# Later remainder splits, a merged frequency column, and attention's value product ahead of the output projection

## The chip, the cores and the metric

The kernel runs on one core of a Trainium2 chip. A core has a matrix engine (PE in the profile; its weight loads are listed apart as PEld), a vector engine (DVE), a scalar engine (ACT), a general engine (POOL), and SP, which here issues nearly all DMA transfers. The engines run side by side, each through its own instructions in order, and wait for one another on semaphores. Matmuls write to PSUM, from where DVE or ACT take the results away. The metric is the device time of one execution in microseconds; a time given for a kernel is the median of its runs.

## The reference

One encoder layer is applied to a prompt of 256 tokens and to a sample of 2048 tokens, both of width 1024, with the same weights. The inputs and outputs are float32:

```python
def encoder_layer(x, w_in, rpb, w_fourier, b_fourier, g_pre, g_na, g_f, w_out, g_post):
    h = rms_norm(x, g_pre)
    proj = h @ w_in                       # 1024 -> 6 * 512
    q, k, v, z_a, u_f, z_f = split(proj)
    y_a = neighbourhood_attention(q, k, v, rpb)
    y_f = fourier_mix(u_f, w_fourier, b_fourier)   # real part of a 2-D FFT, then 512 x 512
    mixed = concat([rms_norm(y_a, g_na) * silu(z_a), rms_norm(y_f, g_f) * silu(z_f)])
    out = mixed @ w_out                   # 1024 -> 1024
    return x + rms_norm(out, g_post)
```

Attention is local: tokens lie on a grid 64 wide, each query sees a window of 8 rows and 16 columns, with a bias from a table. There are 8 heads of 64.

## The kernel before, in words

**Arithmetic.** A float32 product is made of three faster passes. Each operand is split into a high part `h` (a rounded copy, made by ACT) and a remainder `l = x - h` (made by DVE); `mm3` (lines 171 to 173) then issues `h*h`, `h*l` and `l*h` into one PSUM accumulation.

**Stage 1, input projection.** First the value and Fourier columns of the first tokens, then a loop over 16 blocks `b` of 128 output columns for the prompt's 256 tokens (kinds z_f, z_a, k, q). In pass `b` of this loop, `b_raw(b + 2)` splits the weights of the block after next (ACT copy L577, DVE subtraction L578), `n_scale` and `n_sum` prepare operands of the sample, and `n_first(j)` splits operand `j` of the sample: one ACT copy (L444) and one DVE subtraction (L445) of 128 x 2048 elements. Then come 24 matmuls of 256 columns.

**The seven products.** The sample is projected by a scheme of seven products per 2 x 2 block in place of eight, so there are seven operands `j` = 0 to 6. `vu(0, ...)` runs it for the value and Fourier columns in 14 steps, in the order of `j` = 0, 0, 1, 1, 2, 2, 3, 3, 4, 4, 5, 5, 6, 6. Each step is 12 matmuls of 512 columns. `op_split(j)` (L493/L494) splits the weight side of operand `j`; `hooks` is a dictionary from step to further work of the other engines, put ahead of that step's matmuls: `n_first`, `rows_load`/`rows_square` (L305, squares of later token rows, on ACT, behind a DMA), `w_load`, `w_sums`, `a_split`. A step's results are added on DVE (L521). After `vu(0)` the rest of the sample's projection follows, then the second half of the sample.

**Stage 2, Fourier.** `stage2(gq, zg, c)` is called for `gq` 0 to 3 and `c` 0 to 4. It makes four small products of 64 columns each, one per `g`, into one PSUM tile `pab` of 256 columns (two PSUM buffers of tag `b` and one of tag `c` are used in turn). For `gq == 0` a further product with one column, the middle frequency, goes into its own tile `pny` of tag `a`; its weights are in the small constant `dnyq`. `split_ab` takes each tile away as high part and remainder (L997, L998, and L1012, L1014 for `c == 4`).

**Stage 3, attention with the Fourier half's output projection.** After the Fourier product `y` (L1258) there are 36 groups of queries, nine for each of four pairs of heads; group 0 of each nine is the prompt's. The loop runs over steps `k`. In step `k` the matrix engine issues, in this order: `transp` of group `k-2` (transposes the softmax weights into four PSUM tiles `ptb[0]` to `ptb[3]`, L1485, from where DVE and ACT copy them to SBUF, L1489), then `scores` of group `k` (L1179; one of its four tiles is `ptb[0]`). In even steps with a group `g`, the "long steps", two halves of an output projection tile follow: `f_mm(.., 0)` into `ptb[2]` and `f_mm(.., 1)` into `ptb[3]`, 12 matmuls of 512 columns each (L1425). `f_evac(.., 0)` takes `ptb[2]` away on DVE (L1459), `f_evac(.., 1)` takes `ptb[3]` away on ACT (L1456). Last comes `pv` of group `k-2`, the product of softmax weights and values (L1508), into a PSUM tile of tag `c` that has one buffer; DVE multiplies its result by the gate (L1528) and, in the next step after its transposes, ACT squares it (L1532, L1536). The softmax of a group runs on DVE (L1201, bias and maximum), ACT (L1206, exponentials) and POOL (L1213, normalisation) in the steps between.

The transposes fill `ptb[0]` and `ptb[1]` first and `ptb[2]` and `ptb[3]` after them:

```python
for b, ch in enumerate(g["ch"]):
    for j, c in enumerate(ch):
        for h in range(2):
            for y, (c0, nk) in enumerate(c):
                nc.tensor.transpose(ptb[2 * b + y][:nk, x:x + 64], ...)
```

**Stage 4** is the attention half's projection, the last norm and the residual.

**What sets the order.** On PE the order is that of the program throughout. On ACT, DVE, POOL and SP it is the program's order in stage 1 and from attention on (`manual_schedule(engines=MAN)`); in stage 2 and most of the Fourier product a planner orders these four.

Of the kernel before, what the change touches and what calls it, by code (L numbers as in the profile page):

```python
# [10 lines left out]
F32 = mybir.dt.float32  # L11
# [34 lines left out]
def constants():  # L46
    c = {}
    c["ident"] = np.eye(128, dtype=np.float32)
    n1 = np.arange(128)
    f1 = np.zeros((128, 128))  # L50
    for k1 in range(64):
        f1[:, 2 * k1] = np.cos(2 * np.pi * ((k1 * n1) % 128) / 128)
        f1[:, 2 * k1 + 1] = np.sin(2 * np.pi * ((k1 * n1) % 128) / 128) if k1 else (-1.0) ** n1
    c["f1"] = f1.reshape(32, 4, 128).transpose(1, 0, 2).reshape(128, 128)
    nrm = 1.0 / np.sqrt(2048 * 64)
    n2 = np.arange(16)
    d = np.zeros((128, 16, 128))
    for g in range(16):
        for kl in range(4):
            k1 = 4 * g + kl  # L60
            for k2 in range(16):
                if k1:
                    k = k1 + 128 * k2
                elif k2 < 8:
                    k = 128 * k2
                else:
                    k = 64 + 128 * (k2 - 8)
                co = np.cos(2 * np.pi * ((n2 * k) % 2048) / 2048) * nrm
                si = np.sin(2 * np.pi * ((n2 * k) % 2048) / 2048) * nrm
                ca = k2 * 4 + kl  # L70
                cb = 64 + ca
                r0 = (kl * 2) * 16 + n2
                r1 = (kl * 2 + 1) * 16 + n2
                if k1:
                    d[r0, g, ca] = co
                    d[r1, g, ca] = -si
                    d[r0, g, cb] = si
                    d[r1, g, cb] = co
                else:
                    r = r0 if k2 < 8 else r1  # L80
                    d[r, g, ca] = co
                    d[r, g, cb] = si
    c["d2"] = d
    dn = np.zeros((128, 4))
    dn[:16, 0] = ((-1.0) ** n2) * nrm
    dn[:, 2] = np.arange(128) % 32 != 0
    c["dnyq"] = dn
    n = np.arange(256)[:, None]
    k = np.arange(129)[None, :]
    ang = 2 * np.pi * ((n * k) % 256) / 256  # L90
    f256 = np.concatenate([np.cos(ang), np.sin(ang)], axis=1) / np.sqrt(256 * 64)
    c["f256"] = f256.reshape(4, 2, 32, 258).transpose(0, 2, 1, 3).reshape(128, 2, 258)
    f = np.arange(64)
    sl = np.arange(32)
    cs = np.zeros((128, 2, 64))
    for b in range(2):
        rows, cols = slice(64 * b, 64 * b + 64), slice(32 * b, 32 * b + 32)
        ang = 2 * np.pi * ((f[:, None] * sl[None, :]) % 64) / 64
        cs[rows, 0, cols] = np.cos(ang)
        cs[rows, 1, cols] = np.where(sl == 0, (-1.0) ** f[:, None], np.sin(ang))  # L100
    c["cs"] = cs
    cm = np.zeros((128, 2, 32))
    cs_ = np.zeros((128, 80))
    rm = np.zeros((128, 16))
    for p in range(128):
        half, i, qc = p // 64, p // 16 % 4, p % 16
        for b in range(2):
            cb = 2 * b + half
            ws = min(max(16 * cb + qc - 8, 0), 48)
            kc = KP0[cb] + np.arange(32)  # L110
            cm[p, b] = np.where((kc >= ws) & (kc < ws + 16), 0.0, BIG)
        for cb, j in ((0, slice(0, 24)), (1, slice(24, 56)), (3, slice(56, 80))):
            ws = min(max(16 * cb + qc - 8, 0), 48)
            kc = KC0[cb] + np.arange(KW[cb])
            cs_[p, j] = np.where((kc >= ws) & (kc < ws + 16), 0.0, BIG)
        j = np.array(ORD[half])
        rm[p, :11] = np.where((j >= i) & (j < i + 8), 0.0, BIG)
    c["cmask"] = cm.reshape(128, 64)
    c["csmask"] = cs_
    c["rmask"] = rm  # L120
    return {k: np.ascontiguousarray(v.astype(np.float32)) for k, v in c.items()}
# [54 lines left out]
def build(tc, A, O):  # L176
# [31 lines left out]
    invt = cst.tile([128, 18], F32, name="invt")  # L208
    invf = cst.tile([128, 18], F32, name="invf")
    inva = cst.tile([128, 18], F32, name="inva")  # L210
    dnyq = cst.tile([128, 4], F32, name="dnyq")
    cm = cst.tile([128, 80], F32, name="cm")[:, :64].rearrange("p (b x) -> p b x", b=2)


# [226 lines left out]
    def n_first(j):  # L441
        src = nq[((0, 0), (1, 0), (0, 0), (0, 1), "t3", (1, 0), (1, 1))[j]]
        h, l = bnew[0, j] = [k8(F32R, "x" + x) for x in "hl"]
        nc.scalar.copy(h, src)  # L444
        nc.vector.tensor_tensor(out=l, in0=src, in1=f_(h), op=ALU.subtract)  # L445
# [297 lines left out]
    for b in range(16):  # L743
        kind, blk = divmod(b, 4)
        if b < 10:
            wz_load(1)
        if b in (0, 2):
            n_load((b // 2, 1))
        if b == 10:
            op_load(0)  # L750
        if b == 12:
            op_load(1)
        if b < 14:
            b_raw(b + 2)
        if b < 8:
            x, y = divmod(b, 2)
            n_scale(None, *divmod(x, 2)[::-1], range(2 * y, 2 * y + 2))
        elif b < 12:
            n_sum(b - 8)
        if b in (3, 5, 12, 13):  # L760
            n_first((3, 5, 12, 13).index(b))
        if b > 13:
            op_split(b - 14)
        p = mmt(512)[:, :TP]
        wh, wl = wb.pop(b)
        for k in range(KC):
            mm3(nc, p, wh[:, k], wl[:, k], hp_[:, k], lp_[:, k], k == 0, k == KC - 1)
        o = st.tile([128, 256], F32, tag="f", name="f", bufs=3)
        if kind == 1:
            v = [(o, p)]  # L770
        elif kind == 3:
            v = [(o[:, 128 * x:128 * x + 128].rearrange("p (x r c) -> p r x c", x=2, c=16),
                  p[:, 128 * x:128 * x + 128].rearrange("p (r x c) -> p r x c", x=2, c=16)) for x in range(2)]
        else:
            v = [(o.rearrange("p (r b c) -> p b r c", b=2, c=32), p.rearrange("p (b r c) -> p b r c", b=2, c=32))]
        for d, i in v:
            nc.scalar.activation(d, i, AF.Silu if kind < 2 else AF.Copy, scale=-0.125 if kind == 3 else 1.0)
        if kind < 2:
            nc.sync.dma_start(zD[kind, blk * 128:blk * 128 + 128, :TP], o)
        else:  # L780
            nc.sync.dma_start((kD if kind == 2 else qD)[blk, :, :TP], o)
# [14 lines left out]
    def at(i, f, *a):  # L796
        hooks.setdefault(i, []).append(call(f, *a))

    for x in range(4, 7):
        at(3 * x - 12, n_first, x)  # L800
    for x in range(4):
        at(2 * x + 1, rows_load, x + 5)
        at(2 * x + 4, rows_square, x + 5)
# [19 lines left out]
    for i in range(16):  # L823
# [48 lines left out]
        for j in range(7):  # L872
# [28 lines left out]
            if sg == 0:  # L901
                x, y = divmod(7 * (pr - 1) + j, 14)
# [113 lines left out]
    def stage2(gq, zg, c):  # L1016
        m = int(c in (2, 3))
        np_ = 96 if c == 4 else 128
        x = (gq * 5 + c) % 3 == 2
        p = ps.tile([np_, 4, 64], F32, tag="c" if x else "b", name="pab", bufs=1 if x else 2)  # L1020
        for g in range(4):
            dft(p[:, g, :], c, [(zg[g], d2[gq // 2][:, (gq % 2) * 4 + g, m * 64:m * 64 + 64])])
        split_ab(gq, c, lambda a: a[:, :1024].rearrange("p (k q g l) -> p q g k l", k=16, q=4, g=4)[:, gq],
                 p.rearrange("p g (k l) -> p g k l", l=4))
        if gq == 0:
            p = ps.tile([np_, 1], F32, tag="a", name="pny")
            dft(p, c, [(zg[0], dnyq[:, m:m + 1])])
            split_ab(gq, c, lambda a: a[:, 1024:1025], p)
        if gq == 2:
            p = ps.tile([np_, 129], F32, tag="a", name="pup")  # L1030
            dft(p, c, [(up[:, t], f256[:, t, 129 * m:129 * m + 129]) for t in range(2)])
            split_ab(gq, c, lambda a: a[:, 1025:1154], p)
# [6 lines left out]
    def pq(m):  # L1039
# [7 lines left out]
        for b, p in enumerate(pp):  # L1047
            h, l = PQ[m][0][:, b], PQ[m][1][:, b]
            if m == 0:
                split_ps(h, l, p)  # L1050
                continue
            t = sm.tile([128, 512], F32, name="wt%d" % b)
            nc.scalar.copy(t, p)
            nc.scalar.dma_start(wr32[16 * b:16 * b + 16:4], t[::32])
            keep = dnyq[:, 2:3]
            nc.scalar.activation(h, p, AF.Copy, scale=keep)
            nc.vector.scalar_tensor_tensor(out=l, in0=p, scalar=keep, in1=h.bitcast(F32), op0=ALU.mult,
                                           op1=ALU.subtract)
# [514 lines left out]
    for k in range(2, len(G) + 2):  # L1573
# [32 lines left out]
        else:  # L1606
# [4 lines left out]
            if g:  # L1611
# [10 lines left out]
                    ys_mul(ftiles[x + 1])  # L1622
                if x < 16:
                    ys_load(ftiles[x + 2])
                f_mm(ftiles[x], 0)
            else:
                soft(p, 1)
# [20 lines left out]
                f_evac(ftiles[x], 1)  # L1648
        if pr < 3 and i == 7:
            mask_p(pr + 1)  # L1650
        pv(f)
        if k == 12:
            pq_.close()
        if k + 1 < len(G):
# [133 lines left out]
```

## Time and profile before

| what | value |
|---|---|
| median of 3 runs | 938.73 us (937.64 to 939.05) |
| the profiled execution's own time | 937.48 us |
| its span from first to last instruction | 935.7 us |
| PE / PEld / DVE / ACT / POOL busy | 925.3 / 774.5 / 669.9 / 469.8 / 332.0 us |
| granted TensorE clock | 0.999 |
| 16-block prompt loop ends, `vu(0)` begins | 121.5 us into the span |
| stage 2 begins | 553.2 us |
| the 17 long steps with their followers | 612.3 to 819.5 us |

A row of the timeline gives the start in the span, the duration (both us), engine, line, operation, `out<-in`, tile shape and count; in brackets the idle time of that engine before it and what ended it. Matmuls are pipelined: a 512-column matmul shows a duration of 389 ns, while the next one starts some 227 ns after it, so that distances between starts tell more than durations.

### The profile page before, as it was taken

The numbers are of one execution on the slowest core, as the hardware profiler recorded it, in microseconds if no ns is written. First come the engines' busy times: TensorE is split into PE (matmuls) and PEld (weight loads), VectorE is DVE, ScalarE is ACT, GpSimd is POOL, SyncE is SP. The second block draws the span as 40 slices with busy tenths as digits, with TensorE's granted clock in tenths as the row PEclk, the third lists the DMA queues.
The fourth block names the chain that finished last, engine by engine and source line by source line (L and its number), as shares of the span: only waits on it lengthen the run. The fifth ranks groups of instructions, "written<-read, shape, count | busy, mean of one in ns | idle before, by whom it ended". The sixth has DMA issues, their size and how long they took to land.

```text
span 935.7 us, 18895 instructions
## 1 busy us (share of the span) xinstructions
PE 925.3 (99%) x6790; PEld 774.5 (83%) x6790; DVE 669.9 (72%) x1308; ACT 469.8 (50%) x1038; POOL 332.0 (35%) x337
## 2 busy tenths in 40 slices
PE   9999999999999999999999999999999999999997
PEld 7889988888888888888888888978788887888886
DVE  6487997688864967597666645677665666659997
ACT  5856577623332743233334425667655666654443
POOL 3200002436650300363333200445456565525444
PEclk9999999999999999999999999999999999999999
DMA  9899777468573999758888789888779899879993
GB/s 323 329 360 400 217 253 281 158 246 314 201 288 151 352 400 359 265 209 316 294 310 286 273 287 309 295 262 257 245 248 274 264 300 283 255 237 377 341 340 128
DMA packets 144829, 264.04 MB, mean 282 GB/s; under 512 B 21784, under 2 KB 84632, under 8 KB 141984
## 3 DMA queue, kind: packets, MB, share of 16 engines
q1 hardware_dynamic: 144576, 262.81, 80.9%
q8 instruction: 54, 0.88, 0.4%
q14 instruction: 39, 0.32, 0.1%
q10 hardware_dynamic: 160, 0.02, 0.0%
HBM read 174.75 MB, written 95.35 MB: 289 GB/s over the span
## 4 chain that ended last, share of the span: by engine, by line
PE 94%; DMA 3%; DVE 2%; issue 1%; ACT 0%; DVEq 0%; SPq 0%
PE mm L172 18%; PE mm L173 18%; PE mm L171 17%; PE ptb L1425 10%; PE po L1425 10%; PE pv L1508 5%; PE ptb L1485 3%; PE s L1179 3%; PE pab L1005 2%; PE ptb L1179 2%; DMA woD<-wo 1%; PE py L171 1%; PE py L173 1%; PE py L172 1%; PE pf L1425 1%
## 5 line engine op out<-in xcount | busy, mean ns | idle before, releaser
L171 PE MATMUL mm<-xh,wa 128*128 128x512 f32 x448 | 174.4, 389 | 0.0
L173 PE MATMUL mm<-xh,wa 128*128 128x512 f32 x448 | 174.3, 389 | 0.0
L172 PE MATMUL mm<-xl,wa 128*128 128x512 f32 x448 | 174.3, 389 | 0.0
L548 POOL TENSOR_TENSOR ws<-wr 128x512 f32<-128x512 f32 x16 | 22.2, 1386 | 259.3 <-DMA wr<-wz 246.2
L171 PEld LDWEIGHTS mm<-xh,wa 128*128 128x128 f32 x448 | 84.1, 188 | 17.5
L173 PEld LDWEIGHTS mm<-xh,wa 128*128 128x128 f32 x448 | 84.1, 188 | 17.4
L172 PEld LDWEIGHTS mm<-xl,wa 128*128 128x128 f32 x448 | 84.1, 188 | 17.4
L1425 PE MATMUL po<-w,yh 128*128 128x512 f32 x280 | 86.8, 391 | 0.0
L1425 PE MATMUL ptb<-wo,yh 128*128 128x512 f32 x272 | 86.7, 400 | 0.0
L1213 POOL TENSOR_SCALAR w<-w,m 128x352 f32<-128x352 f32 (+4 forms) x136 | 75.4, 572 | 30.4 <-PE s L1179 14.0
L563 DVE TENSOR_TENSOR wa<-wr,wa 128x512 fp32r<-128x512 f32 x60 | 57.7, 969 | 30.6 <-ACT wa L562 30.3
L1206 ACT ACTIVATE w<-w,m 128x352 f32<-128x352 f32 (+4 forms) x136 | 69.9, 521 | 12.5 <-DVE m L1201 12.1
L861 DVE TENSOR_TENSOR f<-u,mm 128x512 f32<-128x512 f32 x64 | 43.6, 681 | 34.1 <-PE mm L173 29.5
L172 PE MATMUL mm<-vl,xh 128*128 128x512 f32 x168 | 65.6, 390 | 0.4 <-DVE vl L494 0.4
L171 PE MATMUL mm<-vh,xh 128*128 128x512 f32 x168 | 65.4, 389 | 0.0
L173 PE MATMUL mm<-vh,xl 128*128 128x512 f32 x168 | 65.4, 389 | 0.0
L1425 PEld LDWEIGHTS ptb<-wo,yh 128*128 128x128 f32 x272 | 49.3, 188 | 14.8 <-ACT sqa L1536 3.4
L1425 PEld LDWEIGHTS po<-w,yh 128*128 128x128 f32 x280 | 52.3, 188 | 11.0
L562 ACT CAST wa<-wr 128x512 fp32r<-128x512 f32 x60 | 36.5, 617 | 42.7 <-PE mm L173 16.8
L1508 PEld LDWEIGHTS pv<-pt,v 96*64 96x64 f32 (+2 forms) x1280 | 45.2, 137 | 11.6 <-issue 6.6
L1425 PE MATMUL po<-w,yl 128*128 128x512 f32 x140 | 54.5, 389 | 0.0
L1425 PE MATMUL ptb<-wo,yl 128*128 128x512 f32 x136 | 53.1, 391 | 0.0
(249 smaller groups left out, 2192.3 us busy)
## 6 DMA issues: line engine op xcount, KB each, us to landing
wr<-wz SPq DMA_DIRECT2D x48, 512.0 KB
vl<-sD SPq DMA_DIRECT2D x20, 512.0 KB
xm<-xm SPq DMA_DIRECT2D x9, 1024.0 KB
oD<-ofs SPq DMA_DIRECT2D x18, 512.0 KB
of<-oD SPq DMA_DIRECT2D x18, 512.0 KB
yr<-yD SPq DMA_DIRECT2D x34, 256.0 KB
zD<-f SPq DMA_DIRECT2D x16, 512.0 KB
woD<-wo SPq DMA_DIRECT2D x16, 512.0 KB
```

The costliest lines, as they stand in the source:

```text
L171: nc.tensor.matmul(out, lh, rh, start=first, stop=False)
L172: nc.tensor.matmul(out, lh, rl, start=False, stop=False)
L173: nc.tensor.matmul(out, ll, rh, start=False, stop=last)
L562: nc.scalar.copy(o[:, 0], src)
L563: nc.vector.tensor_tensor(out=o[:, 1], in0=src, in1=o[:, 0].bitcast(F32), op=ALU.subtract)
L861: nc.vector.tensor_tensor(out=dst(f, b), in0=src(uu[u]), in1=src(p), op=op)
L1179: nc.tensor.matmul(sp[2 * b + h][64 * y:64 * y + 64, j * w:(j + n) * w], g["q"][hs, 128 * b + 64 * y:128 * b + 64 * y + 64], kk[hs, k:k + ...
L1206: nc.scalar.activation(w, w, AF.Exp, bias=m[:, h:h + 1], scale=-1.0, accum_out=m[:, 2 + h:3 + h])
L1213: nc.gpsimd.tensor_scalar(w, w, m[:, 4 + h:5 + h], 1.0, ALU.mult, ALU.mult)
L1425: nc.tensor.matmul(p, (d["l"] if x == 2 else d["h"])[:, c], w(n, int(x == 1), c), start=j == 0, stop=j == 11)
L1485: nc.tensor.transpose(ptb[2 * b + y][:nk, x:x + 64], g["w"][b][ys, h, c0:c0 + nk], ident[ys, ys])
L1508: nc.tensor.matmul(p[hs, b, o], v[:nk, b, x, hs], g["pt"][b][:nk, h, j * 128 + o.start:j * 128 + o.stop], start=first, stop=last)
```

## The change

Three edits that do not depend on one another.

1. **Remainder splits.** `n_first(2)` moves from pass 12 of the prompt loop to pass 13. `n_first(3)` moves from pass 13 to step 1 of `vu(0)`. `n_first(4)`, `(5)` and `(6)` move from steps 0, 3 and 6 of `vu(0)` to steps 4, 7 and 10.
2. **Middle frequency.** The constant `dnyq` grows from 128 x 4 to 128 x 2 x 66 and now holds the 64 columns of `d2` for `g == 0`, the middle frequency as 65th column, and the mask column. The order of `g` is reversed, so that `g == 0` comes last in the `pab` tile, and for `gq == 0` its product has 65 columns instead of 64. The tile `pny` and its matmuls are gone; `split_ab` takes column 256 of `pab` instead.
3. **Values ahead of the projection.** In long steps `pv(f)` stands between the scores and `f_mm(.., 0)`; in the others it stays at the end.

```diff
-        if b in (3, 5, 12, 13):
-            n_first((3, 5, 12, 13).index(b))
+        if b in (3, 5, 13):
+            n_first((3, 5, 13).index(b))
...
-    for x in range(4, 7):
-        at(3 * x - 12, n_first, x)
+    for x in range(3, 7):
+        at(3 * x - 8 if x > 3 else 1, n_first, x)
...
-        p = ps.tile([np_, 4, 64], F32, tag="c" if x else "b", name="pab", bufs=1 if x else 2)
-        for g in range(4):
-            dft(p[:, g, :], c, [(zg[g], d2[gq // 2][:, (gq % 2) * 4 + g, m * 64:m * 64 + 64])])
+        p = ps.tile([np_, 260], F32, tag="c" if x else "b", name="pab", bufs=1 if x else 2)
+        for g in range(3, -1, -1):
+            s = 64 * (3 - g)
+            if gq == 0 and g == 0:
+                dft(p[:, s:s + 65], c, [(zg[g], dnyq[:, m, :65])])
+            else:
+                dft(p[:, s:s + 64], c, [(zg[g], d2[gq // 2][:, (gq % 2) * 4 + g, m * 64:m * 64 + 64])])
...
         if gq == 0:
-            p = ps.tile([np_, 1], F32, tag="a", name="pny")
-            dft(p, c, [(zg[0], dnyq[:, m:m + 1])])
-            split_ab(gq, c, lambda a: a[:, 1024:1025], p)
+            split_ab(gq, c, lambda a: a[:, 1024:1025], p[:, 256:257])
...
                 if x < 16:
                     ys_load(ftiles[x + 2])
+                pv(f)
                 f_mm(ftiles[x], 0)
...
-        pv(f)
+        if k % 2 or not g:
+            pv(f)
```

## Prediction before the run

> **What bounds the kernel now.** I read the page's shares and its chain first, then the busy time by stretch, then the timeline around each edited place.
>
> ```profile
> PE 925.3 (99%) x6790; PEld 774.5 (83%) x6790; DVE 669.9 (72%) x1308; ACT 469.8 (50%) x1038; POOL 332.0 (35%) x337
> PE 94%; DMA 3%; DVE 2%; issue 1%; ACT 0%; DVEq 0%; SPq 0%
> ...
> 613.78:820.30 206.52, 206.07 (x3001) 167.09 (x2997) 134.69 (x499) 131.70 (x416) 114.94 (x179) 1.00 0.87 265
> ```
>
> The matrix engine sets the end: 94% of the chain runs through it, and in the stretch of the long steps (last row: window, its length, then the busy time of PE, PEld, DVE, ACT, POOL) it is busy for 206.07 of 206.52 us. So edit 3, which only reorders that work, can win at most 0.45 us there, and what it can lose is open. Work on other engines counts only where PE comes to wait for it. The three edits touch three separate stretches, so their effects add.
>
> **Edit 3, values ahead of the projection.** This is the largest term. In the old order, one long step and what follows it look like this (PE, then ACT, then the group of all such ACT instructions):
>
> ```profile
> 707.18 0.39 PE L1425 MATMUL ptb<-wo,yl 128*128 128x512 f32 x1
> 707.50 1.59 PE L1508 MATMUL pv<-pt,v 96*64 96x128 f32 x40
> 709.02 0.91 PE L1485 MATMUL ptb<-ident,w 64*128 64x64 f32 x24
> 709.86 0.51 PE L1179 MATMUL s<-kk,q 64*64 64x352 f32 x4
> ...
> 707.60 0.69 ACT L1456 ACTIVATE ofs<-ptb,invf 128x512 f32<-128x512 f32 x1 [1.37 <-PE ptb L1425]
> ...
> L1456 ACT ACTIVATE ofs<-ptb,invf x17: 687/687/687, 619.5 to 818.0; 128x512 f32<-128x512 f32 x17
> ```
>
> The last projection matmul starts at 707.18 and ends at 707.57. Its result is in `ptb[3]`. ACT starts to take it away at 707.60 and is done at 708.29, always 687 ns later, 17 times of 17; ACT sat idle before, so it cannot be earlier. That is 0.79 us after the first value product (707.50). The transposes of the next step write `ptb[3]` again, so they must wait for that evacuation; in the old order the value product of 1.52 us (707.50 to 709.02) lies between and hides it entirely.
>
> In the new order the value product stands ahead of the projection, and the transposes come right behind `f_mm(.., 1)`. That cover is gone. What is left as cover is the first half of the transposes, which go to `ptb[0]` and `ptb[1]`. The 24 transposes take 0.84 us (709.02 to 709.86), the first 12 some 0.42 us. So PE stops for 0.79 + 0.06 - 0.42 = 0.43 us, with 0.06 for the release (the lag is measured below). PE is the bound, and the engine is in order: scores, values and the next step stand behind the waiting transpose, so the stop is lost. Groups with fewer key rows have less cover:
>
> ```profile
> 732.26 0.69 PE L1485 MATMUL ptb<-ident,w 64*96 64x64 f32 x16
> 732.88 0.44 PE L1179 MATMUL s<-kk,q 64*64 64x264 f32 x4
> ...
> 611.05 1.31 PE L1425 MATMUL pf<-wo,y0h 128*128 128x512 f32 x5
> 612.29 0.46 PE L1485 MATMUL ptb<-ident,sc 64*128 64x64 f32 x8
> 612.68 0.66 PE L1179 MATMUL s<-kk,q 64*64 64x256 f32 x8
> ```
>
> With 16 transposes (0.62 us) half is 0.31, and the wait is 0.54; with 8 (0.39 us) half is 0.20, the wait 0.65. The long steps are k = 2, 4, ... 34, seventeen; the transposes behind them are of groups 1, 3, ... 33. Of these two are prompt groups (9, 27; 8 transposes), four lie at the upper edge (1, 11, 19, 29; 16), eleven are full. Sum: 11 x 0.43 + 4 x 0.54 + 2 x 0.65 = 8.2 us.
>
> For the lag between another engine's end and PE's next start there are two rows:
>
> ```profile
> 673.99 0.08 DVE L1201 DVE_READ_ACCUMULATOR2_ANT m<- 128x1 f32 x1
> 674.22 0.68 PE L1485 MATMUL ptb<-ident,w 64*96 64x64 f32 x16 [0.41 <-DVE m L1201]
> ...
> 117.47 1.24 DVE L578 TENSOR_TENSOR wl<-wr,wh 128x1024 fp32r<-128x1024 f32 x1
> 118.77 0.39 PE L173 MATMUL mm<-ph,wl 128*128 128x256 f32 x1 [0.20 <-DVE wl L578]
> ```
>
> DVE's accumulator ends at 674.07, and the transposes that waited start at 674.22: 0.15. A subtraction ends at 118.71 and the matmul starts at 118.77: 0.06. The first is the same instruction as here. With 0.15 in place of 0.06 the sum is 17 x 0.09 = 1.5 us larger, 9.7. I take 8.9, the middle.
>
> The switch from projection to transposes costs the same as that to values: 0.32 us from the last matmul's start, 707.18 to 707.50; the single place where transposes already follow a projection tile shows 0.33 (five matmuls from 611.05 at some 0.23 put the last start near 611.97, transposes at 612.29). So the reordering alone is neutral: up to the next transposes PE changes from one kind of work to another four times in either order.
>
> Does the value product start late in its new place? It needs the copied transposes and its single PSUM buffer, freed by ACT's squares of the previous group.
>
> ```profile
> 713.97 0.39 ACT L1536 ACTIVATE sqa<-pv 128x256 f32<-128x256 f32 x1
> 714.13 0.73 PE L1425 MATMUL ptb<-wo,yh 128*128 128x512 f32 x2
> ```
>
> In step 18 the squares end at 714.36, 0.23 us after PE is through with the scores (714.13, where the projection starts now); with the lag 0.28 us. Projection matmuls never needed that buffer. Step 18 has the shortest scores of the long steps, so this is the worst case; I take 0.3 us for all steps together. DVE's `f_evac(.., 0)` moves back by 1.5 us, and with it the reciprocals behind it and POOL's normalisation:
>
> ```profile
> 705.56 2.44 POOL L1213 TENSOR_SCALAR w<-w,m 128x264 f32<-128x264 f32 x4
> 712.59 0.26 PE L1485 MATMUL ptb<-ident,w 64*96 64x64 f32 x2
> ```
>
> POOL ended that at 708.0, and the transposes that need it came at 712.59: a slack of 4.6 us hides it. The store of the values goes out earlier on SP's queue, ahead of the projection's store, and delays nothing that is needed within the step. Edit 3: **+9.2 us** (8.2 to 10.0).
>
> The Trainium skill, "Perfetto Trace Analysis", section "Matmuls", speaks against this order: independent matmul groups should rotate through PSUM banks so that the evacuation of one overlaps the next group's matmuls. The new order goes back to the bank just filled. Taken alone, without the transposes into the other two tiles, the rule would expose the whole 0.84 us, 17 times, 14.3 us; by the rows half of that is covered.
>
> **Edit 1, remainder splits.** At the end of the prompt loop DVE is late, and PE stops at each pass:
>
> ```profile
> 118.29 0.28 PE L172 MATMUL mm<-pl,wh 128*128 128x256 f32 x1
> 121.50 0.39 PE L171 MATMUL mm<-vh,xh 128*128 128x512 f32 x1
> 122.11 0.50 PE L172 MATMUL mm<-vl,xh 128*128 128x512 f32 x1 [0.21 <-DVE vl L494]
> ...
> 118.61 2.31 DVE L445 TENSOR_TENSOR xl<-nx,xh 128x2048 fp32r<-128x2048 f32 x1
> 120.81 4.65 DVE L494 TENSOR_TENSOR vl<-vr,vh 128x1024 fp32r<-128x1024 f32 x4
> ...
> 141.88 1.05 ACT L305 ACTIVATE xm<-xm 128x1024 f32<-128x1024 f32 x1
> 149.49 1.98 ACT L493 CAST vh<-vl 128x1024 fp32r<-128x1024 f32 x2
> 152.49 1.06 ACT L305 ACTIVATE xm<-xm 128x1024 f32<-128x1024 f32 x1 [1.01 <-DMA xm<-xm]
> ...
> 144.10 2.29 DVE L445 TENSOR_TENSOR xl<-nx,xh 128x2048 fp32r<-128x2048 f32 x1 [2.60 <-ACT xm L305]
> 152.16 2.36 DVE L494 TENSOR_TENSOR vl<-vl,vh 128x1024 fp32r<-128x1024 f32 x2
> ...
> 154.66 0.39 PE L171 MATMUL mm<-vh,xh 128*128 128x512 f32 x1
> ```
>
> Matmuls of 256 columns follow at 0.12 us, so 118.29 to 118.77 holds a stop of 0.36 us (remainder of weights, 117.47); 121.50 to 122.11 and the next start hold 0.38 + 0.11. Without the two `n_first` of 2.2 us, DVE has the weights of pass 15 at 116.5 and the first of `op_split(0)` near 119.8. These stops go: -0.9 us. The stop in pass 14 stays, since DVE still has `n_sum(3)` ahead of it.
>
> But the splits come back where DVE has no room. Operand 6 is needed in step 12. That step started at 154.66 and would now start at 153.8, its first matmul with the remainder 0.45 later, at 154.2. From 144.10 to 154.4 DVE had no idle time: remainder 6 (144.10), two additions, `op_split(5)`, four additions, `op_split(6)` (152.16, 2.36 us). In the new order remainder 5 takes the place of remainder 6, one addition of 0.6 us moves into the idle 2.60 us ahead of 144.10, and remainder 6 comes behind `op_split(6)`, which ends at 153.9. It takes 2.2 us, to 156.1, and PE gets it at 156.2: a wait of 2.0 us. Net **+1.1 us**.
>
> There is a worse form. The old remainder 6 did not start when its ACT copy ended (141.88) but at 144.10, when the squares queued behind the copy were done: its wait named those squares. In step 10 the new order again has squares behind the copy, and they wait for a transfer (152.49). ACT's copy would end at 153.3, the squares at 155.4, remainder 6 at 157.7: a wait of 3.5 us, net +2.6. Remainders 4 and 5 had no such wait; the nearest row, the same instruction, had it. I take +2.0 us, with -0.9 (no wait in step 12 at all) and +2.6 as the ends.
>
> **Edit 2, the merged column.**
>
> ```profile
> 553.99 0.34 PE L1005 MATMUL pny<-dnyq,zg 128*128 128x1 f32 x2
> 554.18 1.08 PE L1005 MATMUL pab<-d,zg 128*128 128x64 f32 x8
> 558.16 0.24 PE L1005 MATMUL pny<-dnyq,zg 128*32 128x1 f32 x6
> 558.33 0.43 PE L1005 MATMUL pab<-d,zg 128*128 128x64 f32 x2
> ...
> 555.08 0.41 DVE L997 CAST abh<-pab 128x256 fp32r<-128x256 f32 x1
> 555.52 0.42 DVE L998 TENSOR_TENSOR abl<-pab,abh 128x256 fp32r<-128x256 f32 x1
> 555.86 0.15 DVE L998 TENSOR_TENSOR abl<-pny,abh 128x1 fp32r<-128x1 f32 x1
> ```
>
> The removed products hold PE for 554.18 - 553.99 = 0.19 us each (0.26 for the fourth, with a short wait), the last, of six narrow ones, for 0.17: 1.0 us in all. A 65th column is nothing beside the weight load that sets the pace. But DVE starts late (555.08) and needs about 0.95 us for each tile's high part and remainder, and the three `pab` buffers now come free only when the extra column is out too (555.86, 0.15). The fourth tile needs the first one's buffer at 555.84 and gets it at 556.06, the fifth needs the second's: of 1.0 us I keep 0.5. Bounds: 0 and -1.0. **-0.5 us**. The larger constant, 67 KB instead of 2, goes out some 350 us earlier.
>
> The Trainium skill, "TensorEngine Tiling (Array Packing)", section "Instruction Overhead", gives a matmul a floor of about 60 cycles; by it the fourteen removed ones would be worth an estimated 0.35 us. The trace, with about 0.1 us for each, decides.
>
> **Sum.** 9.2 + 2.0 - 0.5 = +10.7 us. On the profiled execution, 937.48 us around a span of 935.7, that is 948.2. The median of the runs shown stands 1.25 us above that execution, which would make 949.4. I forecast **949 us**. The forecast's own range, from 8.2 - 0.9 - 1.0 on 937.5 to 10.0 + 2.6 on 938.7: 943.8 to 951.3.
>
> **Rivals.**
>
> *The evacuation stays hidden (other side).* If the transposes behind the projection did not have to wait for `ptb[3]`, edit 3 would cost only its 0.3 us or nothing. What decides is whether ACT ends within 0.42 us of the last projection matmul; for it speaks the place at 612.29, where transposes follow a projection tile without a stop (that tile lies in another PSUM buffer, though); against it the 0.79 us, seventeen times of seventeen. With edit 1 at -0.9, edit 2 at -1.0 and 0.3 left of edit 3, 937.5 - 1.6 = 935.9, 937 with the runs' offset: 8%. With edit 1 at +2.0 and edit 2 at -0.5, 938.7 + 1.8 = 940.5, or no change where edit 1 costs less: 5%.
>
> *The wait sits ahead of all transposes.* If the release is attached to the first transpose of a step and not to the first that writes `ptb[3]`, nothing covers the 0.84 to 0.94 us: 17 x 0.9 = 15.3 us, 955 in all. The first transposes need nothing of that evacuation, which speaks against it. 7%.
>
> *The softmax gets late instead.* Projection and softmax share DVE, so moving `f_mm` back might make the normalised weights late two steps on, and PE would stop there as well, by up to the 1.5 us of the shift where POOL is full (at the four ends of a pair of heads: +6 us). The slack of 4.6 us speaks against it; 4%, 955 or more.
>
> The forecast has 76%. Faster by over 0.2%, about what a measurement of this kernel can tell from no change: 8%; within 0.2%: 5%; slower: 87%. The range that leaves out no more than two in ten, and lets the first two rivals in part of the way, is 942.5 to 954.
>
> **What would show it.** In the changed profile, each long step should end with transposes right behind L1425, and in their middle a gap of 0.4 to 0.6 us on PE, released by ACT L1456, some 9 us in total. Around 154 there should be one wait of 2 us or more in the twelfth step of `vu(0)`, released by DVE L445, and no stop at 118.3 or 121.5. Stage 2 should start its second quarter about half a microsecond earlier after its own start. The prediction is wrong if the waits of PE on L1456 sum to less than 5 us, or if the transposes show no gap.

## The result and the profile after

The changed kernel takes **969.52 us** (965.49 to 973.8, four runs) against 938.45 us for the kernel before beside it: a ratio of 1.0329, 95% interval 1.0302 to 1.0356. It is slower, as forecast, but by 31 us where 10.7 had been summed. The profiled execution took 967.28 us around a span of 965.5. In the changed file the lines of the prompt loop and of `vu` stand one later, those of attention three later: L445 is L446, L1456 is L1459, L1485 is L1488, L1425 is L1428, L1508 is L1511.

First the page: engine totals, and the granted clock in 40 slices of 24 us.

```profile
PE 940.9 (97%) x6776; PEld 785.3 (81%) x6776; DVE 668.0 (69%) x1308; ACT 469.8 (49%) x1038; POOL 332.1 (34%) x337
...
PEclk9999999999999999999999978999999999999999
```

PE is less densely busy (97% for 99%), and there is something that no step of the prediction had: around the 24th slice the matrix engine's clock was not fully granted. The view by stretch says where (window, length, busy time and count of PE, PEld, DVE, ACT and POOL, then the granted clock, the DMA share and GB/s):

```profile
157.50:164.50 7.00, 3.89 (x11) 2.77 (x10) 7.00 (x6) 2.95 (x7) 6.30 (x3) 0.76 0.15 55
561.30:567.20 5.90, 4.87 (x61) 4.58 (x59) 4.97 (x17) 3.14 (x5) 0.52 (x1) 1.00 0.73 259
567.20:587.70 20.50, 20.50 (x143) 19.60 (x142) 6.13 (x18) 5.11 (x16) 1.26 (x1) 0.50 0.85 300
631.65:850.10 218.45, 210.84 (x3005) 169.33 (x2997) 132.77 (x499) 131.75 (x416) 113.63 (x179) 1.00 0.82 250
```

Three stretches carry the loss. In the twelfth step of `vu(0)` PE worked 3.89 of 7 us, half of that time at half clock. Stage 2 began at 561.3 us, PE stood still for a sixth of its first 5.9 us, and then the clock was at half for 20.5 us. The long steps take 218.45 us where the row of before had 206.52; there the clock is full. Compared start by start with the trace of before, PE is 8.1 us late at the start of stage 2, 17.9 at its end, 29.8 after the long steps, and it stays there. Of the 8.1 us, 2.2 had arisen by 102 us, ahead of every edited place; there the profiled executions of all kernels of this study lie between -0.7 and +2.2 us around that of before, whether or not they hold an edit ahead of stage 2, so that this part is not put down to the change.

The waits of PE (what waited, on what: us in total, times, the longest):

```profile
PE ptb L1488 <- ACT ofs L1459: 4.9, 17, 0.5
PE mm L174 <- DVE xl L446: 3.1, 1, 3.1
PE ptb L1428 <- issue: 2.2, 1, 2.2
...
PE mm L173 <- DVE vl L491: 1.3, 1, 1.3
```

The first row is the predicted one, seventeen times. Its 4.9 us is a lower figure than what was lost, since the modelled ends of the matmuls overlap the wait; the starts say more. In the third, PE stops for 2.4 us by starts at 825 us, between two projection matmuls. "Issue" names nothing that it waited for, but the trace has a load of instructions there (queue q8, 16 KB, 825.40 to 826.41), and PE goes on at 827.69, 1.28 us after its end. The timeline of one long step and its follower, PE and then ACT:

```profile
743.66 0.39 PE L1428 MATMUL ptb<-wo,yl 128*128 128x512 f32 x1
743.99 0.63 PE L1488 MATMUL ptb<-ident,w 64*128 64x64 f32 x13
744.83 0.53 PE L1488 MATMUL ptb<-ident,w 64*72 64x64 f32 x11 [0.22 <-ACT ofs L1459]
...
744.09 0.69 ACT L1459 ACTIVATE ofs<-ptb,invf 128x512 f32<-128x512 f32 x1 [2.62 <-PE ptb L1428]
```

ACT takes the bank away from 744.09 to 744.78; the transposes stop in their middle and go on at 744.83, 0.05 us later. The distances between starts at these seventeen places exceed the usual one by 0.40 to 0.64 us, 8.0 us in sum.

Two places of `vu(0)`, PE, DVE and POOL of the changed kernel:

```profile
150.48 0.39 PE L172 MATMUL mm<-vh,xh 128*128 128x512 f32 x1
152.17 0.50 PE L173 MATMUL mm<-vl,xh 128*128 128x512 f32 x1 [1.30 <-DVE vl L491]
157.75 0.39 PE L173 MATMUL mm<-vl,xh 128*128 128x512 f32 x1
161.25 0.80 PE L174 MATMUL mm<-vh,xl 128*128 128x512 f32 x1 [3.11 <-DVE xl L446]
161.84 0.63 PE L172 MATMUL mm<-vh,xh 128*128 128x512 f32 x1
162.27 0.63 PE L173 MATMUL mm<-vl,xh 128*128 128x512 f32 x1
...
148.09 2.29 DVE L446 TENSOR_TENSOR xl<-nx,xh 128x2048 fp32r<-128x2048 f32 x1 [3.63 <-ACT xh L445]
157.83 3.36 DVE L446 TENSOR_TENSOR xl<-nx,xh 128x2048 fp32r<-128x2048 f32 x1
...
159.12 3.21 POOL L549 TENSOR_TENSOR ws<-ws,wr 128x512 f32<-128x512 f32 x1
```

The tenth step waits 1.46 us for `op_split(5)`, which stood behind remainder 5 (148.09). The twelfth waits 3.27 us for remainder 6. Behind that wait matmuls of 512 columns follow at 0.43 us instead of 0.23: the clock is at half, for 3.4 us from 161.0. The stops at 118.3 and 121.5 are gone.

Stage 2's first tiles:

```profile
563.69 0.39 PE L1006 MATMUL pab<-dnyq,zg 128*128 128x65 f32 x2
564.69 0.85 PE L1006 MATMUL pab<-d,zg 128*128 128x64 f32 x6 [0.61 <-DVE abl L999]
565.38 0.39 PE L1006 MATMUL pab<-dnyq,zg 128*128 128x65 f32 x2
...
566.84 3.51 PE L1006 MATMUL pab<-d,zg 128*128 128x64 f32 x17 [0.42 <-PE pab L1006]
```

By starts the fourth column tile waits 0.77 us for its bank and the first tile of the second quarter 0.49. After that seventeen matmuls take 3.51 us, where the row of before at 558.33 had two in 0.43 and about 0.11 us from one to the next: half clock.

### The profile page after: what moved, and what is told of

It is laid out like the page before. It is cut to its first block, busy times and chain, and to the rows that moved or that the text cites. A ratio compares the mean times of both kernels' runs of the same rounds, so it can differ in the third digit from the quotient of the medians.

```text
span 965.5 us, 18877 instructions
## 1 busy us (share of the span) xinstructions
PE 940.9 (97%) x6776; PEld 785.3 (81%) x6776; DVE 668.0 (69%) x1308; ACT 469.8 (49%) x1038; POOL 332.1 (34%) x337
## 4 chain that ended last, share of the span: by engine, by line
PE 44%; DMA 6%; SPq 2%; DVE 2%; ACT 2%; issue 1%; POOL 1%; DVEq 0%; POOLq 0%; ACTq 0%
PE po L1428 10%; PE ptb L1428 8%; PE pv L1511 4%; PE mm L174 3%; PE mm L172 3%; PE mm L173 3%; PE pab L1006 2%; PE ptb L1488 2%; DMA wr<-wz 2%; PE s L1182 2%; DMA mt<-tr 2%; PE ptb L1182 1%; ACT ofs L1459 1%; PE py L172 1%; PE py L174 1%
## 5 line engine op out<-in xcount | busy, mean ns | idle before, releaser
L1428 PE MATMUL ptb<-wo,yh 128*128 128x512 f32 x272 | 87.0, 400 | 2.2 <-issue 2.2
L1428 PE MATMUL po<-w,yh 128*128 128x512 f32 x280 | 86.7, 391 | 0.0
L564 DVE TENSOR_TENSOR wa<-wr,wa 128x512 fp32r<-128x512 f32 x60 | 59.7, 1001 | 36.1 <-ACT wa L563 36.1
L1428 PEld LDWEIGHTS po<-w,yh 128*128 128x128 f32 x280 | 52.3, 188 | 11.0
L1428 PEld LDWEIGHTS ptb<-wo,yh 128*128 128x128 f32 x272 | 49.4, 188 | 12.9 <-issue 2.5
L1511 PEld LDWEIGHTS pv<-pt,v 96*64 96x64 f32 (+2 forms) x1280 | 45.2, 137 | 11.7 <-ACT sqa L1539 6.3
L1428 PE MATMUL po<-w,yl 128*128 128x512 f32 x140 | 54.5, 389 | 0.0
L1428 PE MATMUL ptb<-wo,yl 128*128 128x512 f32 x136 | 53.1, 390 | 0.0
```

The lines of the kernel that those rows point to most:

```text
L564: nc.vector.tensor_tensor(out=o[:, 1], in0=src, in1=o[:, 0].bitcast(F32), op=ALU.subtract)
L1428: nc.tensor.matmul(p, (d["l"] if x == 2 else d["h"])[:, c], w(n, int(x == 1), c), start=j == 0, stop=j == 11)
L1511: nc.tensor.matmul(p[hs, b, o], v[:nk, b, x, hs], g["pt"][b][:nk, h, j * 128 + o.start:j * 128 + o.stop], start=first, stop=last)
```

## The experiments

The theory after this profile: the three edits add; edits 1 and 2 each make PE stop, and the stops take the clock down; edit 3 loses what was predicted. Each run below was timed beside the kernel before (938.05 to 938.75 us in the four sets).

**One edit at a time.** Three kernels hold one edit each, as in the diff above.

> Edit 1 alone: the four norms one after the other at later steps of the remainder pass, the rest as before. Additive theory: the stops at 118 and 121 us are gone (-0.9), the tenth step waits about 1.5 us for its split, the twelfth about 3.3 us for the sixth remainder's low half, and the granted clock drops to half for one stretch of about 3.4 us behind that wait, which costs about 1.6 more: 4 to 6 us slower than before, 942.5 to 945. Prediction's theory: +2.0, 940.5, with no drop of the clock. Rival (the early slowdown is the rows' or the constants' changed layout, not this edit): within 1 us of before.

Measured: 945.14 us, 1.007 (1.0044 to 1.0097). Edit 1 alone, PE's timeline:

```profile
149.97 0.50 PE L172 MATMUL mm<-vl,xh 128*128 128x512 f32 x1 [1.65 <-DVE vl L490]
...
159.05 0.79 PE L173 MATMUL mm<-vh,xl 128*128 128x512 f32 x1 [3.10 <-DVE xl L445]
```

and the view by stretch behind the second wait:

```profile
157.90:164.70 6.80, 5.65 (x13) 4.46 (x14) 6.80 (x7) 2.28 (x4) 5.21 (x3) 0.50 0.21 80
```

Both waits are there (1.81 and 3.26 us by starts), and the clock is at half for 6.8 us from 157.9, of which 5.7 lie behind the second wait and cost half of that, 2.8 us. With the stops of 0.95 us gone: 1.81 + 3.26 + 2.8 - 0.95 = 6.9. The additive theory had the places right and the size 1 to 3 us too low.

> Edit 2 alone: the groups of a column tile in reverse order, the middle frequency's column as the 65th of the last group's matmuls, the constant grown from 4 to 132 columns. Additive theory: two waits of 0.6 to 0.8 us in the first two quarters of the second stage, and then the granted clock at half for about 20 us, which costs 9 to 10: about 948. Rival (the half clock needs the phase that edit 1's delay gives, since the window of the clock runs free): the waits of 1.4 us in sum alone, no half clock in the second stage, 939 to 940.5. Prediction's theory: -0.5, 938.2.

Measured: 951.71 us (947.79 to 955.41), 1.0139 (1.0092 to 1.0186). Edit 2 alone, PE's timeline and then the view by stretch:

```profile
556.81 0.85 PE L1006 MATMUL pab<-d,zg 128*128 128x64 f32 x6 [0.61 <-DVE abl L999]
...
558.97 8.48 PE L1006 MATMUL pab<-d,zg 128*128 128x64 f32 x57 [0.42 <-PE pab L1006]
```

```profile
553.00:595.40 42.40, 41.14 (x335) 37.31 (x333) 19.89 (x60) 16.65 (x38) 1.77 (x2) 0.76 0.71 236
```

The kernel before has full clock over the same stretch:

```profile
553.00:595.40 42.40, 42.40 (x406) 39.38 (x405) 24.70 (x83) 23.20 (x54) 6.35 (x9) 1.00 0.92 312
```

In edit 2 there are the same two stops, 0.78 and 0.49 us by starts, and half clock from 558.8 to 579.3 us (0.76 over this stretch). Edit 1 is not needed for it, so that rival falls. The four runs had mean granted clocks of 0.979 to 0.987, the slower ones the lower clocks: how long the clock stays down varies.

> Edit 3 alone: in long steps the value products go out ahead of the projection. Prediction's theory: the 17 waits of the transposes on ScalarE's evacuation, 8.0 us, and 0.3 to 1.4 us of value products that wait for their bank: 947 to 949, with a granted clock of 1.0 in the attention. Rival (with all edits together the attention slowed by 11.9 us because the stages before had left another phase of the queues): less than 6 us slower than before.

Measured: 948.71 us, 1.0112 (1.0082 to 1.0142), clock full in attention. The losses of the three, 7.1 + 13.7 + 10.7 = 31.4 us, agree with the 31.1 of the whole change: the edits add, as far as runs tell of which those with edit 2 spread over 8 us.

**Is it the bank?** Edit 3 with the projection's second half in another bank:

```diff
+        elif n:
+            p = ps.tile([128, 512], F32, tag="a", name="pf", bufs=3)
         else:
-            p = ptb[2 + n]
+            p = ptb[2]
```

> Edit 3 with one more change: the projection's second half is accumulated in a bank of the three that the scores use, not in the transposes' last bank. If the waits come from that bank being reused, as predicted, the 17 waits on ScalarE's evacuation are gone and the time is about 8 us under edit 3 alone: 939 to 941, less what the scores lose by having one bank fewer for a while (up to 3 us). Rival (the transposes wait since values ahead of the projection put the next softmax's products late, whatever bank): within 2 us of edit 3 alone.

Measured: 941.07 us, 1.0035 (1.0022 to 1.0047), 7.6 us under edit 3 alone. The waits of PE in attention, edit 3 alone:

```profile
PE ptb L1485 <- ACT ofs L1456: 4.9, 17, 0.5
PE pv L1508 <- issue: 1.8, 2, 1.1
```

and with the other bank, and then its timeline of PE at the end of a long step:

```profile
PE pv L1510 <- issue: 0.9, 1, 0.9
PE pv L1510 <- DVE pt L1491: 0.6, 1, 0.6
PE pv L1510 <- ACT sqa L1538: 0.2, 1, 0.2
```

```profile
723.89 0.39 PE L1425 MATMUL pf<-wo,yl 128*128 128x512 f32 x1
724.21 0.91 PE L1487 MATMUL ptb<-ident,w 64*128 64x64 f32 x24
```

The seventeen waits are gone, all 24 transposes run through behind the last projection matmul, and the time falls by what the starts had put on those waits. So the loss is the reuse of `ptb[3]`, not the order as such. What stays, 3.0 us, is what the order costs besides. By starts 2.1 us of it lie at the value products of three steps: 0.7 for their transposed weights (635.73), 0.3 for their own bank (717.01), and 1.1 on "issue" in their middle (692.05). There too a load of instructions ended 1.4 us before PE went on. In the four kernels with edit 3 five stops on "issue" exceed 0.3 us, each 1.3 to 1.5 us behind the end of such a load, and the kernel before has none in attention; no run tests the load as the cause.

**Does idle time take the clock down?** Three kernels. In the first, edit 2 gets seven products more, which nobody reads, where PE waits:

```diff
+        for r in range({(0, 3): 4, (1, 0): 3}.get((gq, c), 0)):
+            if r == 0:
+                pf_ = ps.tile([128, 64], F32, tag="a", name="fill")
+            dft(pf_, 0, [(zgs[0][r], d2[0][:, r, :64])])
         p = ps.tile([np_, 260], F32, tag="c" if x else "b", name="pab", bufs=1 if x else 2)
```

> Edit 2 with seven products more, whose results nobody reads, in the two places where PE waits: four ahead of the fourth column tile of the first quarter, three ahead of the first tile of the second quarter. VectorE's work and the release of the banks are as in edit 2. Theory (it is PE's idle time there that takes the clock down): PE is busy through the waits, the granted clock stays at 1.0, and only about 1.5 us of the 13.7 is left: 938.5 to 940.5. Rival (something else in edit 2 takes the clock down, for example the lower number of products in the whole stage): half clock as in edit 2, 948 to 953.

Measured: 939.0 us, 0.9999 (0.9987 to 1.0011). PE's timeline and the view by stretch:

```profile
555.72 1.06 PE L1006 MATMUL fill<-d,zg 128*128 128x64 f32 x8
556.61 0.83 PE L1006 MATMUL pab<-d,zg 128*128 128x64 f32 x6
```

```profile
553.00:595.40 42.40, 42.09 (x400) 38.84 (x399) 24.87 (x83) 22.64 (x53) 5.25 (x7) 1.00 0.88 302
```

The tile comes no earlier (0.89 us after the fill's start), yet the clock stays at 1.0, and 12.7 us are gone though PE has more to do.

The second is the kernel before, with no merged column; its first low half is computed four times more (same values), so that banks come free later:

```diff
+        if gq == 0 and c == 0:
+            dv = lambda a: a[:, :1024].rearrange("p (k q g l) -> p q g k l", k=16, q=4, g=4)[:, gq]
+            for _ in range(4):
+                nc.vector.tensor_tensor(out=dv(AC[c][1]), in0=p.rearrange("p g (k l) -> p g k l", l=4),
+                                        in1=dv(AC[c][0]).bitcast(F32), op=ALU.subtract)
```

> The kernel before with the low half of the very first column tile subtracted four times more by VectorE (same values), 1.7 us more of its work, so that banks of the second stage come free later and PE stops there for about 1 us in sum, without any merged column. Theory (stops alone are enough): the granted clock drops to half for 10 to 35 us, 943 to 953. Rival (stops of this size do not move the clock): 938.5 to 940, clock at 1.0.

Measured: 950.03 us, 1.0115 (1.0083 to 1.0147). PE's timeline and the view by stretch:

```profile
555.93 1.08 PE L1005 MATMUL pab<-d,zg 128*128 128x64 f32 x8 [0.59 <-DVE abl L998]
557.63 1.00 PE L1005 MATMUL pab<-d,zg 128*32 128x64 f32 x24 [0.45 <-DVE abh L997]
558.62 8.72 PE L1005 MATMUL pab<-d,zg 128*128 128x64 f32 x58
```

```profile
553.00:595.40 42.40, 41.36 (x302) 36.44 (x303) 16.65 (x47) 14.52 (x34) 1.26 (x1) 0.56 0.65 219
```

Two stops (0.75 and 0.60 us by starts), half clock from 557.8 to 595.4 us. Idle time is enough, and edit 2's column is not needed.

The third removes the waits of the first quarter, by giving two tiles the banks that the separate column had:

```diff
+        if gq == 0 and c > 2:
+            p = ps.tile([np_, 260], F32, tag="a", name="pab")
+        else:
+            p = ps.tile([np_, 260], F32, tag="c" if x else "b", name="pab", bufs=1 if x else 2)
```

> Edit 2 with the last two column tiles of the first quarter in banks that the separate column's tiles had before, so that no tile of that quarter waits for another's column to be taken away. Theory (the merged column holds each bank until VectorE has come to two operations of one element, PE stops 1.5 us in two places, and the granted clock drops because of these stops): the waits are under 0.3 us, the clock stays at 1.0 and the prediction's gain is there, -0.5 to -1.0 against the kernel before: 937 to 937.8. Rival (the clock drops because the column's own products, which kept PE active, are gone): the waits are gone, the clock is still at half for some 20 us, 946 to 949.

Measured: 938.61 us, 0.9996 (0.9984 to 1.0009). In the profile the clock stayed up in stage 2, but one stop of 0.79 us by starts was left, at the second quarter:

```profile
559.63 5.45 PE L1006 MATMUL pab<-d,zg 128*128 128x64 f32 x64 [0.73 <-PE pab L1006]
```

Nine of its ten runs lie within 937.85 and 940.28 us. The tenth took 952.1 at a mean granted clock of 0.983 and is left out of the ratio; it was not profiled, so whether this stop took its clock down is not shown. With that tile too in one of those banks:

```diff
-        if gq == 0 and c > 2:
+        if gq == 0 and c > 2 or gq == 1 and c == 0:
```

> Edit 2 alone with three tiles in the separate column's banks. Theory: the five tiles are 0.2 us shorter each (-0.8 to -1.05), no wait over 0.3 us and no half clock in the second stage, 937.4 to 938.2 where the kernel before has 938.5. Rival (the time that the column leaves is taken by the next wait): 938.5 or more.

Measured: 938.47 us (937.35 to 940.04), 1.0002 (0.9992 to 1.0011).

```profile
557.36 0.60 PE L1006 MATMUL pab<-d,zg 128*32 128x64 f32 x18
...
558.02 5.47 PE L1006 MATMUL pab<-d,zg 128*128 128x64 f32 x64
```

No stop is left, each of the first four tiles is 0.19 to 0.22 us shorter than before (start by start), and no run falls out of line. The 0.8 us can be seen in the trace and is too small for the timing.

**Can edit 1 be put right?** Three other places for the four splits; the first:

```diff
-        at(3 * x - 8 if x > 3 else 1, n_first, x)
+        at(2 * x - 5, n_first, x)
```

> Edit 1 with the sixth split three steps earlier (the four norm splits at steps 1, 3, 5 and 7, where edit 1 has 1, 4, 7 and 10). Theory: the two waits of edit 1 (1.8 us in the tenth step, 3.3 us in the twelfth) come from the last split's late place, and the half clock behind them from the waits; both go, the stops at 118 and 121 us stay away, so the time is 0.5 to 1.0 under the kernel before: 937 to 937.7. Rival (fourteen steps cannot hold four splits wherever they stand, since the squares and the weights' splits share ScalarE): at least 3 us slower than before.

Measured: 938.9 us, 1.0005 (0.999 to 1.0019). PE's waits on a remainder here:

```profile
150.07 0.50 PE L172 MATMUL mm<-vl,xh 128*128 128x512 f32 x1 [1.13 <-DVE vl L490]
```

The twelfth step's wait is gone and with it the half clock, but the stop in the tenth step stays at 1.29 us by starts. So 0.95 is won and 1.3 lost. The other two places stood in kernels with edit 2 mended as above and no edit 3: splits at steps 1, 2, 4, 6,

```diff
-        at(3 * x - 8 if x > 3 else 1, n_first, x)
+        at((1, 2, 4, 6)[x - 3], n_first, x)
```

> The kernel before with edits 1 and 2, mended: the four norm splits at steps 1, 2, 4 and 6, the last of them where it stood before; and three tiles of the second stage (two of the first quarter, the first of the second) in the banks that the separate column had. No edit 3. Theory: stops at 118 and 121 us gone (-0.95), no wait in the tenth and twelfth step, five column tiles 0.2 us shorter (-1.05), no wait of PE in the second stage over 0.3 us, clock at 1.0: -2.0 against the kernel before, 936 to 937. Rival (each gain has its cost in another place that these edits only move): within 0.5 us of the kernel before, as with the two mended edits alone.

and at steps 2, 4, 6, 8, each right behind the weights' split of its step:

```diff
-        at((1, 2, 4, 6)[x - 3], n_first, x)
+        at(2 * x - 4, n_first, x)
```

> Edits 1 and 2 mended in another way: the four norm splits at steps 2, 4, 6 and 8, each right behind the weights' split of its step and ahead of the squares; three tiles of the second stage in the separate column's banks. Theory (what costs is a weights' split that stands behind a norm split and the squares on ScalarE): the fifth weights' split comes no later than before, so no wait in the tenth and twelfth step, and -1.9 in sum, 936.5 to 937.5. Rival (ScalarE has no room for four norm splits in these steps, in any order, since steps 4 to 9 ask 6.3 us of it for every 5.4 us of matmuls): a wait of 1 us or more in steps 8 to 12, 938 to 942.

Measured: 940.71 us, 1.0022 (1.0009 to 1.0035), and 943.41 us, 1.0059 (1.0044 to 1.0074). PE's timeline of the first, then PE's and ACT's of the second:

```profile
154.06 0.77 PE L173 MATMUL mm<-vl,xh 128*128 128x512 f32 x1 [2.76 <-DVE vl L491]
```

```profile
159.64 0.79 PE L173 MATMUL mm<-vl,xh 128*128 128x512 f32 x1 [3.31 <-DVE vl L495]
...
141.76 1.05 ACT L494 CAST vh<-vl 128x1024 fp32r<-128x1024 f32 x1 [2.40 <-DMA vl<-sD]
```

Each order makes another split late (2.9 us in the tenth step, 3.5 us in the twelfth, by starts), and the clock falls to half for 3.4 us behind it. None of the four orders tried, edit 1's among them, beats the one before. Why exactly ScalarE has no room is not settled: it has gaps in these steps, but they are waits for transfers (2.40 us for a weight operand's landing at 141.76), and everything behind stands in line.

**The whole change, mended** (edits 1 and 2 as at steps 1, 2, 4, 6, edit 3 with the other bank):

> The whole change with all three mended: edits 1 and 2 as in the other run of this call, edit 3 with the projection's second half in one of the scores' banks. Theory (all of the change's loss lies in the waits named): 30 of the 31 us are gone, what stays of edit 3 is the 2 to 3 us of value products that wait, less the 2.0 gained: 938 to 940. Rival (the slower attention or the clock has a cause not named yet): over 943.

Measured: 943.4 us, 1.0052 (1.0033 to 1.0071). Of the 31 us, 26 are gone and 4.6 stay. In the profiled execution, compared start by start with before, edit 1's place loses 3.4 us (its tenth step stops for 2.8, with 3.4 us of half clock behind it, less the 0.95 gained), attention loses 2.1, and stage 2 wins 0.2. No version found beats the kernel before beyond what the timing can tell.

## Why the prediction was wrong, point by point

- **What bounds.** Right: PE sets the end. "What it can lose is open" was the half that mattered. That the three effects add was right too, as far as the spread of the runs tells.
- **Edit 3, transposes behind the projection (8.9 us, from 8.2 by the short lag).** Right in place, cause and size: 8.0 us by starts, 7.6 by the run with another bank. The lag is the short one, 0.05 us. The prediction set its own failure at under 5 us of such waits, and the row says 4.9; the starts and the run decide that the row counts too little.
- **Edit 3, value products (0.3 us).** Nearly right. The wait for the bank in step 18 is 0.28 us, as it was worked out (736.80), and the products of one more step start 0.19 late (653.47). What the sum did not have is the stop of 2.4 us at 825 us on "issue", behind a load of instructions; its cause stays open.
- **Edit 1, the stops that go (-0.9 us).** Right, 0.95.
- **Edit 1, the twelfth step (2.0 to 3.5 us).** Measured 3.27, near the worse form, for a partly different reason: remainder 6 does start behind `op_split(6)`, at 157.83, but takes 3.36 us, not 2.2. That the number comes near the worse form is luck.
- **Edit 1, the tenth step (nothing).** This step failed: "remainder 5 takes the place of remainder 6". Remainder 5 could not take the place at 144.10, since its ACT copy came behind squares; in edit 1 alone it started at 145.89, and `op_split(5)` behind it was late by 1.81 us (1.46 in the whole change). The queue on ACT in the new order was looked at for remainder 6 alone.
- **Edit 2, the products saved (-1.0 us).** Right: 0.2 us per tile. **The buffers (0.5 of it lost):** the place was right, the size not; the tile's bank waits not for one operation of one element but for those that the planner put between, 1.3 us in two places. The second quarter starts 5.55 us after the stage, where before it was 5.18: 0.37 later, not half a microsecond earlier.
- **The term that was missing.** On this step the forecast failed: the prediction treated a stop of PE as lost time and no more. Every stop was priced at its own length, with the clock of 0.999 of before taken for granted. Edit 2's 1.3 us of stops brought 20.5 us of half clock, which cost 9.4 us (17.9 less 8.1 makes 9.8 lost over stage 2, of which 1.3 are the stops, and 0.9 had been saved); edit 1's brought 1.6 us in the whole change and 2.8 alone. In the profiled execution, 29.8 us over that of before, these 11.0 are the larger part of the 19.1 us by which the sum was short. Of the others, 2.7 lie in attention (11.9 for 9.2), 2.2 ahead of every edited place, 1.8 in edit 1's stops (3.8 net for 2.0) and 0.9 in edit 2's (0.4 net for -0.5); 0.5 is not placed.
- **Rivals.** None of the three came: the evacuation was not hidden, the wait stood in the middle of the transposes, and the softmax was not late.

## What to carry to other kernels

A stop of PE is not priced by its length alone: ask what the clock does behind it, above all in a stretch of small matmuls, and look at the granted clock by stretch before looking for anything else. Before merging a small result into a larger tile, look at what releases the tile's bank; a result that is taken away in two parts holds it until the later one. When two pieces of PE work change places, ask which bank the next piece writes, and who still reads it.

## What the runs showed of the hardware

**The clock falls after short stops, and stays down.** In the profiled executions:

| kernel | stops of PE, by starts | half clock |
|---|---|---|
| before | none in stage 2 | none |
| edit 2, filled | 0.47 us once | none |
| edit 2, two banks | 0.79 us once | none |
| edit 2 | 0.78 and 0.49 us within some 3 us | 20.5 us |
| whole change, stage 2 | 0.77 and 0.49 us within some 3 us | 20.5 us |
| before, with delays | 0.75 and 0.60 us within some 3 us | 37.6 us |
| edit 1 at steps 1, 3, 5, 7 | 1.29 us, 512-column matmuls | none |
| whole change, at 825 us | 2.4 us, 512-column matmuls | none |
| edits 1 and 2, steps 1, 2, 4, 6 | 2.9 us, 512-column matmuls | 3.4 us |
| whole change, `vu(0)` | 1.46 and 3.27 us, 512-column matmuls | 3.4 us |
| edit 1 | 1.81 and 3.26 us, 512-column matmuls | 6.8 us |

The stretches of half clock are multiples of 3.4 us. Among wide matmuls the clock is back after one or two of them; in stage 2, most of whose products have 64 columns, it stayed down for 6 to 11, although PE shows as busy for nearly all of it. The same products run at full clock from end to end where no stop interrupts them. Each row is one profiled execution; whether it matters where a stop falls between two changes of the clock was not tested.

The Trainium skill, "TensorE: Matmul & The Clock Gate", section "What's actually happening", describes a gate that halves the clock by activity in a free-running window of 3413 ns; the multiples agree. Its section "Why this matters for your kernels" advises against idle gaps of more than about 3 us; among the wide matmuls that agrees (2.4 us did nothing, 2.9 did), in stage 2 the measurement differs, where two stops of 0.5 to 0.8 us were enough.

**VectorE and GpSimd slow each other.** In the whole change remainder 6 takes 3.36 us while POOL's `ws` operation at 159.12 runs, and POOL's takes 3.21. Apart, each is shorter: POOL's operation in the trace of before, and the same remainder with the splits at steps 2, 4, 6, 8, where no POOL operation runs beside it:

```profile
157.75 1.29 POOL L548 TENSOR_TENSOR ws<-ws,wr 128x512 f32<-128x512 f32 x1
...
153.76 2.29 DVE L446 TENSOR_TENSOR xl<-nx,xh 128x2048 fp32r<-128x2048 f32 x1 [2.11 <-ACT xm L306]
```

The Trainium skill, "GPSIMD Engine Reference", section "1. Specifications", names contention with VectorE instructions that have two SBUF inputs, which this subtraction has; the rows agree.
